# A mixture-of-experts stage: experts two at a time in the two halves of the array's columns, with unsplit fp32 weights

## The chip, the cores and the metric

The kernel runs on one core of a Trainium2 chip. The metric is device time in microseconds (us) of one execution. The kernel before takes 1715.51 us, the median of three runs (1713.52 to 1718.09). One execution was profiled; it took 1711.88 us.

## The reference, cut to what matters

One block of a network over 256 tokens of width 2048, all in float32: an adaptive norm, one projection to three mixers (stick-breaking attention, a state-space layer, a chunked mLSTM), a gated merge, an output projection with a residual, and then the part that the change is about, a hierarchical mixture of experts. A token takes one of 4 groups, and in that group its best 2 of 8 experts:

```python
g_logits = (t @ w_group) + b_group
g_idx = jnp.argmax(g_logits, axis=-1)
e_in_group = jnp.take_along_axis(e_logits, g_idx[:, None, None], axis=1)[:, 0]
top_v, top_i = lax.top_k(e_in_group, TOP_K)
top_w = jax.nn.softmax(top_v, axis=-1) * g_w
...
hid = jax.nn.silu(jnp.einsum('td,edf->tef', t, w1)) * jnp.einsum('td,edf->tef', t, w3)
y = jnp.einsum('tef,efd->td', hid * gates[:, :, None], w2)
...
x = x + gate2 * y          # then a final RMS norm
```

There are 32 experts. Each has w1 and w3 (2048 x 256) and w2 (256 x 2048), 6 MiB in float32, 192 MiB for all of them. The routing depends on the data, so every expert's weights are read.

## The kernel before, in words

Everything up to the output projection (`wo`, which ends at about 1081 us of the profile) is the same in both kernels and is not described here. Weights come from memory in tiles of 1 MiB (128 partitions x 2048 float32), issued on SyncE's queue, and each tile is a buffer of a ring.

**Split products.** A plain float32 product is not used for the large matrices. `split` makes a high part (`hi`, a rounded copy in the type fp32r, made by ScalarE at L134) and a low part (`lo = x - hi`, made by VectorE at L136) of half a tile, 128x1024 at a time. `mm3` (L146 to L148) then issues three fp32r products, high x high, high x low and low x high.

**The experts.** The 256 tokens are put into 128 slots per group: `sel_group` builds a one-hot selection matrix from each token's rank in its group, and `Gather` (rows, scale, turn, finish) picks the tokens by a product with it, scales them, transposes them into 16 chunks of 128 features x 128 slots, modulates and splits them into `XG`. All 8 experts of a group then run over all 128 slots of that group, one expert after the other; a slot whose token did not choose the expert has gate 0. Per expert there are 16 steps (chunks of the 2048 features) of `mm_in`, each with a 128x512 operand that holds w1 and w3 side by side, and 8 steps of `mm_out` (2 chunks of the hidden width x 4 blocks of 512 output columns). One step is one `mm3`, three products. Between the two stand `hidden` (silu, gate, transpose) and `hidden_split`. At the end of a group the result is gated (`gate_rows`, `gate_low`), brought back to the tokens by a product with the transposed selection (`combine_mm`) and added to `x1` (`combine_add`). The gather of the next group and the combine of the last one are spread over the experts of a group in the loop at the end.

**Buffers and order.** `moe_raw` hands out the weight buffers: six in two pools (`st`, which the loads of `wo` use too, and `pd`), and for some of the early tiles the place of other tensors (`Y0`, `Y1`, `H1`). A tile can be loaded again when VectorE has made its last low part. A scheduler orders the instructions of each engine, except in two stretches written out by hand (`manual_schedule`): the router between `wo` and the first expert, and the last expert with the final norm. In the router's stretch the rank of a token in its group needs the group's one-hot `goh` alone; the choice of the two experts is worked out behind it and is needed for the gates alone. If a group has more than 128 tokens, a branch (`overflow`) computes the rest.

Of the kernel before, what the change touches and what calls it, by code (L numbers as in the profile page):

```python
# [18 lines left out]
P = 128  # L19
D = 2048  # L20
# [24 lines left out]
def kernel(ctx: ExitStack, tc: tile.TileContext, A, out, dbg=None):  # L45
# [75 lines left out]
    def split(src, shape, name, part=None, hl=None, buf=None):  # L121

        if part == 1:
            nc.vector.tensor_tensor(out=hl[1], in0=src, in1=hl[0].bitcast(F32), op=ALU.subtract)
            return hl
        hi = buf[0] if buf else ring["pool"].tile([P, 1024], F32R, tag="hi", bufs=ring["bufs"], name=name + "h")
        lo = buf[1] if buf else ring["pool"].tile([P, 1024], F32R, tag="lo", bufs=ring["bufs"], name=name + "l")
# [7 lines left out]
        if part is None:  # L135
            nc.vector.tensor_tensor(out=lv, in0=src, in1=hv.bitcast(F32), op=ALU.subtract)  # L136
# [1080 lines left out]
    slots = {}  # L1217
# [15 lines left out]
    def sel_group(g):  # L1233
        if "sel" not in slots:
            slots["sel"] = pd.tile([P, 2, 4, 128], F32R, tag="wrg", name="sel")
        sel = slots["sel"]
        for tt in range(2):
            V.tensor_scalar(sel[:, tt, g, :], iota, rank[:, tt:tt + 1], oh[:, tt, g:g + 1], op0=ALU.is_equal,
                            op1=ALU.mult)

    def slot_r2(sl, nm):

        pt = psum("ms", f"r2p{nm}")
        for tt in range(2):
            nc.tensor.matmul(pt[:, :1], lhsT=sl[tt].bitcast(F32), rhs=r2[:, tt:tt + 1], start=(tt == 0),
                             stop=(tt == 1))
        r = pd.tile([P, 1], F32, tag="r2s", bufs=2, name=f"r2s{nm}")
        V.tensor_copy(out=r, in_=pt[:, :1])
        return r

    class Gather:


        def __init__(self, sl, nm):
            self.sl, self.nm = sl, nm

        def norms(self):
            if isinstance(self.sl[0], tuple):
                self.sl = [slots["sel"][:, tt, g, :] for tt, g in self.sl]
            self.r = slot_r2(self.sl, self.nm)  # L1260

        def rows(self, j):
            self.pt = psum("ms", f"xg{self.nm}{j}")
            for i in range(2):
                for tt in range(2):
                    nc.tensor.matmul(self.pt, lhsT=self.sl[tt], rhs=xs[i][:, tt, 512 * j:512 * j + 512],
                                     start=(i == 0 and tt == 0), stop=(i == 1 and tt == 1))

        def scale(self, j):
            self.x = pd.tile([P, 512], F32, tag="xgr", bufs=2, name=f"xgr{self.nm}{j}")  # L1270
            nc.scalar.activation(self.x, self.pt, AF.Copy, scale=self.r)

        def turn(self, j):
            self.pT = psum("ms", f"xgT{self.nm}{j}").rearrange("p (k s) -> p k s", k=4)
            for kk in range(4):
                transpose(self.pT[:, kk, :], self.x[:, kk::4], P)

        def modulate(self, j, h):
            for kk in range(4):
                k = 4 * j + kk  # L1280
                if kk % 2 == 0:
                    nc.scalar.activation(h[:, kk, :], self.pT[:, kk, :], AF.Identity, bias=modc[:, 3, k:k + 1],
                                         scale=G2[:, k:k + 1])
                else:
                    V.tensor_scalar(h[:, kk, :], self.pT[:, kk, :], G2[:, k:k + 1], modc[:, 3, k:k + 1],
                                    op0=ALU.mult, op1=ALU.add)

        def finish(self, j, XG):
# [487 lines left out]
```

## Time and profile before

| | us |
|---|---|
| median of 3 runs | 1715.51 |
| the profiled execution | 1711.88 |
| its span, first to last instruction | 1710.1 |
| `wo` ends, router begins | 1080.6 to 1086 |
| first product of an expert | 1097.2 |
| last product of an expert ends | 1692.6 |

Over the whole span PE is busy 94% of the time, VectorE 85%, ScalarE 56%. A matmul's duration in the profile runs from its start to the end of its pipeline, so matmuls overlap, and the distance from one start to the next tells what one costs. The weight loads into the array (PEld) are listed apart.

### The profile page before, as it was taken

What the parts mean: (1) busy time and instruction counts of PE and PEld (TensorE: products, weight loads), DVE (VectorE), ACT (ScalarE), POOL (GpSimd) and SP (SyncE); (2) the same over time, 40 slices, a digit from 0 to 9 for tenths busy, and PEclk for the clock granted to TensorE, in tenths of its full rate; (3) what the DMA queues carried; (4) which work ended last, traced back from release to release, by engine and by line L of the source; (5) the groups of instructions that cost most, each with busy time, mean ns of one, the idle gap of its engine ahead of it and who ended that gap; (6) DMA issues with size and microseconds to landing.
All of it is one profiled execution on the core that took longest, in us unless ns stands there. A gap on an engine that the chain in (4) does not pass through costs nothing. (4 is left out here: it accounts for less than half of the span.)

```text
span 1710.1 us, 26968 instructions
## 1 busy us (share of the span) xinstructions
PE 1613.5 (94%) x10568; PEld 1421.2 (83%) x10568; DVE 1452.8 (85%) x2072; ACT 951.4 (56%) x1133; POOL 38.1 (2%) x59
## 2 busy tenths in 40 slices
PE   1999999999998989989999999899999999999996
PEld 1999998888897988979999988678878877777774
DVE  5889997988799999987788556688898998889897
ACT  4454454755533333424444344577887787777775
POOL 1000010100000000000000100000000000000000
PEclk9999999999999999999999999899999999999998
DMA  9998876677777767777988585598899999899993
GB/s 347 351 358 318 264 210 222 202 247 250 273 278 243 255 237 271 265 244 253 321 314 314 195 316 200 187 361 302 287 361 345 322 338 354 320 327 346 346 350 125
DMA packets 172004, 488.24 MB, mean 286 GB/s; under 512 B 13876, under 2 KB 14048, under 8 KB 162272
## 3 DMA queue, kind: packets, MB, share of 16 engines
q1 hardware_dynamic: 168784, 474.32, 78.3%
q0 software_dynamic: 3088, 12.14, 2.2%
q8 instruction: 84, 1.38, 0.3%
q14 instruction: 48, 0.39, 0.1%
HBM read 479.06 MB, written 6.31 MB: 284 GB/s over the span
## 5 line engine op out<-in xcount | busy, mean ns | idle before, releaser
L136 DVE TENSOR_TENSOR w_1l<-w,w_1h 128x1024 fp32r<-128x1024 f32 x127 | 155.1, 1222 | 20.2 <-ACT w_1h L134 20.0
L136 DVE TENSOR_TENSOR w_0l<-w,w_0h 128x1024 fp32r<-128x1024 f32 x128 | 156.4, 1222 | 17.8 <-ACT w_0h L134 16.4
L321 DVE SCALAR_TENSOR_TENSOR accr<-adar,ccol,accr 128x1024 f32<-128x1024 f32 x120 | 153.5, 1279 | 13.5 <-DMA adar<-in_w_ada_dram 12.4
L134 ACT CAST w_1h<-w 128x1024 fp32r<-128x1024 f32 x128 | 134.5, 1051 | 36.4 <-PE h L148 19.5
L134 ACT CAST w_0h<-w 128x1024 fp32r<-128x1024 f32 x128 | 134.2, 1048 | 24.3 <-PE y L148 14.3
L146 PE MATMUL h<-w_0h,XG 128*128 128x512 f32 x256 | 105.5, 412 | 1.4 <-ACT XG L1292 0.9
L147 PE MATMUL h<-w_0l,XG 128*128 128x512 f32 x256 | 103.0, 402 | 3.7 <-DVE w_0l L136 3.3
L147 PE MATMUL h<-w_1l,XG 128*128 128x512 f32 x256 | 102.4, 400 | 0.2
L148 PE MATMUL h<-w_0h,XG 128*128 128x512 f32 x256 | 101.4, 396 | 0.1
L146 PE MATMUL h<-w_1h,XG 128*128 128x512 f32 x256 | 101.4, 396 | 0.0
L148 PE MATMUL h<-w_1h,XG 128*128 128x512 f32 x256 | 101.1, 395 | 0.0
L136 DVE TENSOR_TENSOR w2s_0l<-w,w2s_0h 128x1024 fp32r<-128x1024 f32 x63 | 77.1, 1224 | 9.0 <-ACT w2s_0h L134 8.6
L136 DVE TENSOR_TENSOR w2s_1l<-w,w2s_1h 128x1024 fp32r<-128x1024 f32 x62 | 75.9, 1224 | 7.9 <-ACT w2s_1h L134 6.2
L301 DVE SCALAR_TENSOR_TENSOR acc<-ada,ccol,acc 128x1024 f32<-128x1024 f32 x60 | 76.9, 1282 | 2.7 <-DMA ada<-in_w_ada_dram 1.4
L134 ACT CAST w2s_1h<-w 128x1024 fp32r<-128x1024 f32 x62 | 65.2, 1052 | 23.7 <-PE y L148 16.6
L134 ACT CAST w2s_0h<-w 128x1024 fp32r<-128x1024 f32 x63 | 66.3, 1052 | 16.0 <-PE h L148 15.6
L147 PEld LDWEIGHTS h<-w_0l,XG 128*128 128x128 f32 x256 | 48.1, 188 | 18.9 <-DVE w_0l L136 9.0
L147 PEld LDWEIGHTS h<-w_1l,XG 128*128 128x128 f32 x256 | 48.1, 188 | 16.5 <-DVE w_1l L136 5.8
L146 PEld LDWEIGHTS h<-w_0h,XG 128*128 128x128 f32 x256 | 48.3, 189 | 12.4 <-ACT XG L1292 1.9
L146 PEld LDWEIGHTS h<-w_1h,XG 128*128 128x128 f32 x256 | 48.1, 188 | 11.5
L148 PEld LDWEIGHTS h<-w_0h,XG 128*128 128x128 f32 x256 | 48.1, 188 | 11.2 <-DVE XG L1293 1.3
L148 PEld LDWEIGHTS h<-w_1h,XG 128*128 128x128 f32 x256 | 48.1, 188 | 10.5
(677 smaller groups left out, 5565.2 us busy)
## 6 DMA issues: line engine op xcount, KB each, us to landing
w<-in_moe_w_dram SPq DMA_DIRECT2D x256, 512.0 KB, 4.9
adar<-in_w_ada_dram SPq DMA_DIRECT2D x64, 1024.0 KB, 5.6
w<-in_moe_w_dram SPq DMA_DIRECT2D x64, 1024.0 KB, 5.6
ada<-in_w_ada_dram SPq DMA_DIRECT2D x64, 512.0 KB, 7.1
g_sb_w<-in_w_in_dram SPq DMA_DIRECT2D x16, 1024.0 KB, 5.6
g_ml_w<-in_w_in_dram SPq DMA_DIRECT2D x16, 1024.0 KB, 5.5
g_s_w<-in_w_in_dram SPq DMA_DIRECT2D x16, 1024.0 KB, 5.5
wo_w<-in_w_out_dram SPq DMA_DIRECT2D x16, 1024.0 KB, 5.1
```

Source lines behind the costliest of these rows:

```text
L134: nc.scalar.copy(out=hv, in_=src)
L136: nc.vector.tensor_tensor(out=lv, in0=src, in1=hv.bitcast(F32), op=ALU.subtract)
L146: nc.tensor.matmul(o, lhsT=lhs[0], rhs=rhs[0], start=start, stop=False, **kw)
L147: nc.tensor.matmul(o, lhsT=lhs[0], rhs=rhs[1], start=False, stop=False, **kw)
L148: nc.tensor.matmul(o, lhsT=lhs[1], rhs=rhs[0], start=False, stop=stop, **kw)
L301: nc.vector.scalar_tensor_tensor(acc, raw[:, :, q], cs, acc, op0=ALU.mult, op1=ALU.add)
L321: nc.vector.scalar_tensor_tensor(acc, raw[:, q], cs, acc, op0=ALU.mult, op1=ALU.add)
```

## The change

It replaces the expert stage from the router on. Experts are paired with experts of the same parity: a set is two neighbouring experts (16 sets), a unit is two sets (8 units), and a slot of a set holds a token that chose either of the set's experts. A unit has 64 slots for its first set and 64 for its second, side by side in the 128 columns of the stationary operand. A `Pair` (16 of them, two per unit) runs one expert of each set at the same time: the first in the array's columns 0 to 63, the second in columns 64 to 127 (`tile_position`), each with its own weights streamed and with plain float32 products on the weights as loaded; nothing of the experts is split any more. There is a step of 16 + 8 per pair, with two products in a step. The overflow branch now begins at 64 tokens in a set and is rewritten. The selection now needs both chosen experts, so their choice moves ahead of the rank in the router's stretch. The ring has 11 weight buffers: three of pool `pd`, three of `st`, three that were the split parts of the projections (`hl`), and two in the place of `H1`. `split` now allocates one tile for both parts. The combine keeps its split products.

```diff
     def split(src, shape, name):
-        hi = buf[0] if buf else ring["pool"].tile([P, 1024], F32R, tag="hi", bufs=ring["bufs"], name=name + "h")
-        lo = buf[1] if buf else ring["pool"].tile([P, 1024], F32R, tag="lo", bufs=ring["bufs"], name=name + "l")
+        hi, lo = (lambda t: (t[:, 0], t[:, 1]))(ring["pool"].tile([P, 2, 1024], F32R, tag="hl", bufs=ring["bufs"],
+                                                                  name=name))
...
+    def sel_unit(u):
+        sel = pd.tile([P, 2, 128], F32R, tag="sel", bufs=2, name=f"sel{u}")
         for tt in range(2):
+            for h in range(2):
+                V.tensor_scalar(sel[:, tt, 64 * h:64 * h + 64], iota[:, 0:64], rank[:, tt, 2 * u + h:2 * u + h + 1],
+                                mem[:, tt, 2 * u + h:2 * u + h + 1].bitcast(F32), op0=ALU.is_equal, op1=ALU.mult)
+        return sel
...
+        def finish(self, j):
+            modulate(self.pT.pop(j), j, self.X[:, 4 * j:4 * j + 4, :])
...
     def moe_raw(name):
+        n = ring_n[0] % 11
+        ring_n[0] += 1
+        if n >= 9:
+            if n == 9:
+                h1[:] = [cp.tile([P, 2, 2048], F32, tag="H1", name=name)]
+            return h1[0][:, n - 9]
+        rp, tag = ((pd, "raw"), (st, "raw"), (ring["pool"], "hl"))[n // 3]
+        return rp.tile([P, 2048], F32, tag=tag, bufs=3, name=name)
...
+        def mm(self, o, lhsT, rhs, start, stop):
+            for h in range(2):
+                sl = slice(64 * h, 64 * h + 64)
+                nc.tensor.matmul(o[sl, :], lhsT=lhsT[:, sl], rhs=rhs(h), start=start, stop=stop,
+                                 tile_position=(0, 64 * h), skip_group_check=True)
+        def mm_in(self, j):
...
+            for kk in range(4):
+                k = 4 * j + kk
+                self.mm(self.ph, self.ga.X[:, k, :], lambda h: self.raw[j][h][:, :, kk, :], k == 0, k == 15)
...
-        gm, ohr = first_max(G, 4, iota4, "g", F32R)
+        gm, oh = first_max(G, 4, iota4, "g")
...
+        v1, oh1 = first_max(eg, 8, iota8, "e1")
...
+        v2, oh2 = first_max(e2, 8, iota8, "e2_")
...
+        V.tensor_reduce(out=m4, in_=both2.rearrange("p t (i q) -> p t i q", q=2), axis=AX.X, op=ALU.max)
+        V.tensor_tensor(out=mem.rearrange("p t (g i) -> p t g i", g=4),
+                        in0=m4[:, :, None, :].to_broadcast([P, 2, 4, 4]),
+                        in1=oh[:, :, :, None].to_broadcast([P, 2, 4, 4]), op=ALU.mult)
         prk = psum("ms", "rank")
+        nc.tensor.matmul(prk[:, 0:16], lhsT=lo_r[:, 0], rhs=mem[:, 0, :], start=True, stop=True)
...
+    for n in range(2 * NU - 1):
+        cur = Pair(n, ga)
...
+        for j in range(4):
+            cur.load_in(j)
+        for f in range(2):
+            cur.load_out(f)
+        cur.mm_in(0)
+        cur.mm_in(1)
+        if gat:
...
+            nxt.rows(2 * el)
+            nxt.scale(2 * el)
+        cur.mm_in(2)
...
+        cur.mm_in(3)
+        cur.hidden()
...
+        for c in range(4):
+            cur.mm_out(0, c, py)
...
+        for c in range(4):
+            cur.mm_out(1, c, py)
```

Of the last pair's w2 the two halves of the output columns come one after the other (`load_out`), as with the last expert before, and its steps, the last combine and the final norm stand in the hand-written stretch at the end.

**Where instructions move.** On PE, before, between the router and the first expert's products (`xg` and `xgT` gather and transpose the tokens; `h` is an expert's hidden product; a number behind `w` names expert, chunk and half):

```order
L1465 MATMUL rank<-goh,lo_r 128x4
...
L262 MATMUL xgT_11258<-cst,xgr_11244 128x128 x3
L146 MATMUL h_11265<-w_0_0_0h,XG_11108 128x512 [waits Activation_49]
L147 MATMUL h_11265<-w_0_0_0l,XG_11108 128x512
L148 MATMUL h_11265<-w_0_0_0h,XG_11108 128x512 [waits DVE_49]
...
L262 MATMUL xgT_11311<-cst,xgr_11289 128x128 [waits DVE_49,Activation_49]
```

On PE now, the same place (`w_0` and `w_2` are the two experts of the first pair, `64x512` is a product in one half of the columns):

```order
L1272 MATMUL xg_10964<-xs_10162,sel_10921 128x512 x2
L1272 MATMUL xg_10964<-xs_10163,sel_10921 128x512 x2
L258 MATMUL xgT_10975<-cst,xgr_10969 128x128 x4
L258 MATMUL xgT_10986<-cst,xgr_10980 128x128 x4
L1293 MATMUL gg_11014<-within,sel_10921 128x8 x2
L258 MATMUL selT_11020<-cst,sel_10921 128x128 x2
L1528 MATMUL cnt<-mem,cst 1x16 x2
L1357 MATMUL h_11063<-w_0_0_11032,XG 64x512
L1357 MATMUL h_11063<-w_2_0_11035,XG 64x512
```

The first expert's products stood between the second and the last chunk of the gather; now all four chunks are turned before the first pair's product. Where three products with full columns stood for one step of one expert, two with half the columns stand for one step of two experts.

On SyncE's queue, before, with what each load waits for (`wo_w` are the projection's tiles; DMAHW is an earlier load's end):

```order
L118 DMA wo_w_11109<-in_w_out_dram 128x4x512 [waits DMAHW4_49,DMAHW1_49,DVE_49]
L1332 DMA w_0_0_11119<-in_moe_w_dram 128x1024 [waits DMAHW5_49,DMAHW2_49,DVE_49]
...
L1332 DMA w_1_0_11447<-in_moe_w_dram 128x1024 [waits DMAHW4_49,DVE_49]
...
L1332 DMA w_2_1_11627<-in_moe_w_dram 128x1024 [waits DMAHW1_49,DVE_49]
...
L1370 DMA w_1_0_11644<-in_moe_w_dram 128x2048 [waits DMAHW3_49,DVE_49,Activation_49]
```

And now, behind the last tile of `wo_w`:

```order
L118 DMA wo_w_10797<-in_w_out_dram 128x4x512 [waits DMAHW7_49,DMAHW2_49,DVE_49]
L1337 DMA w_2_1_11041<-in_moe_w_dram 128x1024 [waits DMAHW0_49,DVE_49]
...
L1337 DMA w_0_3_11050<-in_moe_w_dram 128x1024 [waits PE_49]
...
L1337 DMA w_1_0_11172<-in_moe_w_dram 128x1024 [waits DMAHW1_49,PE_49]
...
L1337 DMA w_3_0_11175<-in_moe_w_dram 128x1024 [waits DMAHW3_49,PE_49]
```

Five tiles stood ahead of this place in the queue before and three now. A load of the steady state waited for VectorE, which reads a tile last; now it waits for PE. The first load that needs a tile back from a pair is that of `w_1_0`, the twelfth tile.

## Rows read from the trace of the kernel before

**Rows 1.** Busy time in stretches of the span. Columns: us of the stretch, then busy time and number of instructions of PE, PEld, DVE, ACT and POOL, the granted share of TensorE's clock, the DMA engines' busy share, GB/s.

```profile
1084.70:1095.00 10.30, 7.33 (x26) 6.16 (x26) 7.15 (x33) 4.75 (x8) 0.00 (x0) 0.50 0.80 295
1110.00:1675.00 565.00, 560.68 (x2455) 445.76 (x2456) 506.66 (x524) 436.30 (x508) 0.23 (x1) 1.00 0.92 335
...
1250.00:1300.00 50.00, 49.96 (x220) 39.77 (x219) 47.50 (x49) 40.42 (x47) 0.00 (x0) 1.00 0.99 366
0.00:100.00 100.00, 63.03 (x463) 58.36 (x464) 70.67 (x73) 48.92 (x62) 5.91 (x14) 1.00 0.98 349
```

**Rows 2.** Waits of SyncE's queue in the expert stage (1110 to 1680): who waited for whom, us in total, times, longest.

```profile
SPq L1332 <- DVE w_1l L136: 198.5, 83, 8.9
SPq L1370 <- DVE w2s_1l L136: 114.3, 45, 3.7
```

**Rows 3.** The page's DMA issues of the experts' weights: line, count, KB each, median us from issue to landing.

```profile
w<-in_moe_w_dram SPq DMA_DIRECT2D x256, 512.0 KB, 4.9
...
w<-in_moe_w_dram SPq DMA_DIRECT2D x64, 1024.0 KB, 5.6
```

**Rows 4.** PE's instructions in order of time, in the expert stage: start us, duration us, engine, line, operation. Eight products of an expert, fp32r, 512 columns streamed.

```profile
1396.06 0.40 PE L147 MATMUL y<-w2s_0l,hh 128*128 128x512 f32 x1
...
1397.69 0.40 PE L148 MATMUL y<-w2s_1h,hh 128*128 128x512 f32 x1
```

**Rows 5.** The same view at 397 us, plain fp32 products on the full array. One product makes two records, merged here (x2).

```profile
397.54 0.60 PE L867 MATMUL rest<-sbs,cst 128*128 128x256 f32 x2
397.97 0.38 PE L868 MATMUL rest<-sbs,cst 128*128 128x128 f32 x2
398.19 0.39 PE L869 MATMUL rest<-sbs,cst 128*128 128x128 f32 x2
```

**Rows 6.** The same view at 759 us, plain fp32 products in four groups of 32 columns (128*32): x8 is four products with two records each, one product per column group.

```profile
758.79 0.39 PE L670 MATMUL yc<-u_sb,KB 128*128 128x128 f32 x2
759.10 0.43 PE L675 MATMUL yc<-bu,C 128*32 128x128 f32 x8
759.34 0.40 PE L679 MATMUL yc<-bu,C 128*32 128x127 f32 x8
759.56 0.40 PE L675 MATMUL yc<-bu,C 128*32 128x128 f32 x8
759.78 0.40 PE L679 MATMUL yc<-bu,C 128*32 128x127 f32 x8
760.11 0.38 PE L146 MATMUL g_ml_b<-hT,g_ml_w_1h 128*128 128x256 f32 x1
```

**Rows 7.** Loads of the stationary operand, by source line: count, duration ns min/median/max, first and last start, form (partitions*columns).

```profile
L274 PEld LDWEIGHTS adar<-accr,cst x128: 106/120/130, 371.0 to 939.8; 128*32 128x32 f32 x128
...
L146 PEld LDWEIGHTS h<-w_0h,XG x256: 186/188/202, 1097.2 to 1679.3; 128*128 128x128 f32 x128
```

**Rows 8.** All engines in order of time, from the end of `wo` to the first expert (in brackets: idle time before it and what ended it).

```profile
1080.60 0.39 PE L148 MATMUL wo_b<-wo_w_1h,mh 128*128 128x512 f32 x1
...
1086.33 0.16 DVE L1224 TENSOR_REDUCE gmx<-lg 128x2 f32<-128x8 f32 x1
1086.52 0.17 DVE L1227 TENSOR_TENSOR goh<-lg,gmx 128x8 fp32r<-128x8 f32 x1
...
1087.12 0.17 DVE L1230 TENSOR_TENSOR goh<-goh,gmn 128x8 fp32r<-128x8 f32 x1
...
1087.43 0.34 PE L1465 MATMUL rank<-goh,lo_r 128*128 128x4 f32 x1 [2.03 <-DVE goh L1230]
...
1088.75 0.60 DVE L1238 TENSOR_SCALAR sel<-cst,rank_t,goh 128x128 fp32r<-128x128 f32 x2
...
1090.02 3.76 PE L1266 MATMUL xg<-xs,sel 128*128 128x512 f32 x8
...
1092.16 0.69 ACT L1271 ACTIVATE xgr<-xg,r2s 128x512 f32<-128x512 f32 x1 [4.38 <-PE xg L1266]
...
1094.67 0.46 ACT L1282 ACTIVATE hg<-xgT,modc,G 128x128 f32<-128x128 f32 x1
1095.16 0.41 DVE L1285 TENSOR_SCALAR hg<-xgT,G,modc 128x128 f32<-128x128 f32 x1 [2.17 <-ACT hg L1282]
...
1096.12 0.40 DVE L1285 TENSOR_SCALAR hg<-xgT,G,modc 128x128 f32<-128x128 f32 x1
...
1097.22 0.50 PE L146 MATMUL h<-w_0h,XG 128*128 128x512 f32 x1 [0.94 <-ACT XG L1292]
```

**Rows 9.** The same view at the end of the span.

```profile
1674.77 0.53 POOL L1701 DMA_DIRECT2D fg<-in_final_g_dram  x1 [592.20 <-DVE w2s_1l L136]
...
1681.83 0.38 ACT L1353 ACTIVATE s<-h 128x256 f32<-128x256 f32 x1 [0.80 <-PE h L148]
...
1683.40 0.37 ACT L1363 CAST hh<-hT 128x256 fp32r<-128x256 f32 x1 [0.25 <-PE hT L262]
...
1692.23 0.40 PE L148 MATMUL y<-w2s_3h,hh 128*128 128x512 f32 x1
...
1700.70 5.39 DVE L1746 SCALAR_TENSOR_TENSOR x<-x,r,fg 128x512 f32<-128x512 f32 x8 [0.91 <-DVEq L1571]
1701.48 4.97 SPq L1748 DMA_DIRECT2D out_dram<-x  x8
```

More of the change, by code (lines that the diff above doesn't have):

```diff
@@ L1275, in turn @@
+            x = self.x.pop(j)
             for kk in range(4):
[L1276 to L1286, printed above, removed]
@@ new lines, in back @@
+        def back(self):
+            pt = psum("ms", f"selT{self.u}")
+            for tt in range(2):
+                transpose(pt[:, 128 * tt:128 * tt + 128], self.sel[:, tt].bitcast(F32), P)
+            self.selT = pd.tile([P, T], F32R, tag="selT", bufs=2, name=f"selTs{self.u}")
+            nc.scalar.copy(out=self.selT, in_=pt[:, :T])
+    ring_n = [0]
+    h1 = []
+    def moe_raw(name):
+        n = ring_n[0] % 11
[6 more added lines that the diff above has]
+        return rp.tile([P, 2048], F32, tag=tag, bufs=3, name=name)
@@ new lines @@
+    done = nxt = None
+    for n in range(2 * NU - 1):
+        cur = Pair(n, ga)
+        u, el = cur.u, cur.el
+        gat = u + 1 < NU
+        for j in range(4):
+            cur.load_in(j)
+        for f in range(2):
+            cur.load_out(f)
+        cur.mm_in(0)
+        cur.mm_in(1)
+        if gat:
+            if el == 0:
+                nxt = Gather(u + 1)
+                nxt.norms()
+                nxt.gates()
+            nxt.rows(2 * el)
+            nxt.scale(2 * el)
+        cur.mm_in(2)
+        if gat:
+            nxt.rows(2 * el + 1)
+            nxt.scale(2 * el + 1)
+        cur.mm_in(3)
+        cur.hidden()
+        if done is not None:
+            combine_add(2 * el, combine_mm(done[0], done[1][el][:, 0], u - 1, 2 * el))
+        elif gat:
+            nxt.turn(2 * el)
+        cur.hidden_turn()
+        if done is not None and gat:
+            nxt.turn(2 * el)
+        if gat:
+            nxt.finish(2 * el)
+        if el == 0:
+            py = [psum("mm", f"y{u}_{c}") for c in range(4)]
+        for c in range(4):
+            cur.mm_out(0, c, py)
+        if gat:
+            nxt.turn(2 * el + 1)
+            nxt.finish(2 * el + 1)
+        if done is not None:
+            combine_add(2 * el + 1, combine_mm(done[0], done[1][el][:, 1], u - 1, 2 * el + 1))
+        for c in range(4):
+            cur.mm_out(1, c, py)
+        if el == 1:
+            yp = row_pairs(u)
+            for c in range(4):
+                gate_low(yp[c // 2][:, c % 2], gate_rows(py[c], yp[c // 2][:, c % 2], u, c))
+            done = ga.selT, yp
+            ga = nxt
+            ga.back()
@@ L1700 @@
+    cur = Pair(2 * NU - 1, ga)
+    for j in range(4):
+        cur.load_in(j)
+    for f in range(2):
+        cur.load_out(f)
     fg = pd.tile([P, D], F32, tag="raw", bufs=3, name="fg")
```

517 lines of the change are left out of this document (189 added, 328 removed).

## Prediction

> **What bounds the kernel now.** I read the windows by stage first, then the waits of the load queue, then PE's timeline, because the question is whether the expert stage ends by products or by loads. In the 565 us of that stage PE is busy 560.7, the DMA engines have a share of 0.92 and move 335 GB/s [rows 1]. Busy PE is not PE at its peak, so I take the distance of starts: 1396.06 to 1397.69 over seven products is 0.233 us each [rows 4]. An expert has 24 steps of three products, 32 experts 2304; times 0.233 is 537 us of the 595 from the first product at 1097.2 [rows 8] to the end of the last at 1692.6 [rows 9]. Gather, transposes and combine fill most of the rest. PE is the bound.
>
> The loads are close behind. All experts are 192 tiles of 1.0486 MB, 201.3 MB, in the issues of [rows 3]. The load queue waits for VectorE's low parts, 198.5 us and 114.3 us [rows 2]: the loads run at the pace at which tiles come free, not at their own. Left alone they go faster: 366 GB/s at share 0.99 in 1250 to 1300, and 349 at 0.98 in the first 100 us [rows 1].
>
> **The change part by part.** *The step.* Three fp32r products per expert and step go, 1.40 us for two experts. One plain fp32 product per expert comes. Its price is in [rows 5]: 256 streamed columns take 397.54 to 397.97, 0.43 us for two records; 128 take 0.22. So 512 columns cost 0.86 us. Whether the two halves overlap is the heart of the case. In [rows 6] four products of 128 columns, each in its own quarter of the array's columns, start every 0.22 us (759.34, 759.56, 759.78), the time that one such product takes alone. Four ran in the time of one, so I take two in the time of one: 0.86 us per step of two experts.
>
> *PE per pair.* 24 steps by 0.86 are 20.6 us. Eight gather products and eight of the combine at 0.233 are 3.7. Eight gather transposes and two of the hidden product come to 1.7 (an estimate: 0.11 a record from [rows 5], with the pipeline's start). Norms, gates and the transposed selection are 0.8, estimated. Changing between full and half columns costs about 0.1: 758.79 to 759.10 is 0.31 for one product that takes 0.22, and 759.78 to 760.11 is 0.33 for a wave that takes 0.22 [rows 6]. A pair has five such blocks, so ten changes, 1.0 us. From the start of the silu to the end of the copy of the transposed product there are 1.9 us [rows 9], of which the combine's products cover half. Sum 28.8 us.
>
> *Loads per pair.* Twelve tiles are 12.58 MB. Between 335 and 366 GB/s they take 37.6 to 34.4 us. I take 360, near the faster row, since its packets are these weights' own and the first 100 us carry another matrix: 35.0 us. This exceeds 28.8, so the bound passes from PE to the loads, with 6 us to spare per pair, and the removed splits (1.05 us on ScalarE and 1.22 on VectorE per half tile) are worth nothing beyond the earlier release of tiles. PE releases two tiles at the end of each four steps, 3.4 us after they can start; eleven buffers hold 32 us of loads, so the queue is not starved by it.
>
> The Trainium skill, "DMA: Bandwidth & Descriptors", section Specifications, puts the memory limit of one core at about 358 GB/s. The 366 GB/s over 50 us in [rows 1] lie above it. By the page the stage would end 3 us later than by my 360.
>
> *The start.* The loads are full speed only once tiles come back. Eleven tiles can be loaded before a pair has computed; the last five of them wait for the projection's last product at 1080.6 [rows 8], and at 2.9 us each they are in at about 1096. Then the queue waits for the twelfth. The router grows: the choice of the two experts, its sum and its maximum, 16 small VectorE instructions in a row, come ahead of the rank, at the 0.2 us spacing of 1086.33, 1086.52 and 1087.12 (two intervals there) [rows 8], 3.2 us. A unit's selection is four instructions of 64 columns for two of 128 (0.6 us together), between 0 and 0.6 more; I take 0.5. The gather thus begins at 1090.0 + 3.7 = 1093.7. Before, the first expert's product came 7.2 us after the gather's first (1090.02 to 1097.22), behind two turned chunks; now it stands behind four. A chunk is finished by alternating ScalarE and VectorE, 1094.67 to 1096.52, 1.85 us; with the scaling 2.0 per chunk, and 4.0 for two. First pair product at 1104.9; its first four steps end at 1108.3, and the first two tiles are free. Of this neither end is certain: 1104 if the chunks overlap better, 1112 if the clock, 0.50 of full from 1084.7 to 1095.0 [rows 1], stays there through these steps.
>
> *The stream.* 181 tiles are left, 189.8 MB. At 360 GB/s 527.2 us; at 366, 349 and 335 it is 518.6, 543.8 and 566.6. Add 2 us for the restart (4.9 us from issue to landing under load [rows 3] less the transfer's own share) and 2 us for the final norm's 1 MB, which joins at the end as before [rows 9]. Loads end at 1108.3 + 2 + 527.2 + 2 = 1639.5.
>
> *The tail.* With the last tile in, two blocks of output columns are left, 3.4 us, and one combine between them, 0.9. From the end of the last product to the end of the span is 1710.1 - 1692.6 = 17.5 us [rows 9]; this part keeps its instructions. For a lowered clock in a thinly used stretch I add 1.0. The span ends at 1662.3. The profiled execution is 1.8 us longer than its span, so 1664.1, and lies 3.6 below the median of the runs: 1667.7, said as 1668.
>
> **The rivals.** *The halves do not overlap.* Two products in a step then take 1.72 us, a pair 28.8 + 20.6 = 49.4, the stage 1104.9 + 16 x 49.4 = 1895, with the tail 1913, and 1919 as a median. That is slower by 12%. The kernel would be slower from the point where a step costs over 1.18 us (stage end 1692.6 less 1104.9, over 16, less 8.2 us of other work, over 24). For it: only groups of 32 columns with 128 streamed are seen here, never 64 with 512. Against it: three of three spacings in [rows 6]. 6%.
>
> *Loads of the stationary operand are not hidden.* Each step needs two of them in a row per half. A load of 32 columns takes 0.12 us and one of 128 takes 0.188 [rows 7]; 64 lie between. At 0.188 a pair gains 24 x 2 x 0.188 = 9.0 us, 37.8 in all, and the stage would last 605 us from 1104.9: about 1733 as a median. At 0.12 it is 34.6, just under the loads, and the forecast stands. Against it: in [rows 6] waves of products with fresh stationary operands follow at 0.22, with no room for a load between. 5%. The Trainium skill, "TensorE: Matmul & The Clock Gate", Part 3, says that such a load overlaps with running products only where the row groups differ; here both halves use the same rows, so by that rule this rival is the result, and [rows 6] speak against the rule.
>
> *Loads stay at their present pace or under it.* At 330 GB/s the stream takes 575 us and the median is 1716, no change; at 335 it is 1707. For it: 335 is what the stage shows now, and tiles of a pair are freed two at a time. Against it: the reason for that pace is named in [rows 2] and goes. No change 5%; what lies between 335 and 360 belongs to the forecast.
>
> *PE falls to half its clock through the stage*, since it idles in every pair. Then 24 steps take 41 us and PE is the bound at some 53 us per pair. But a PE that is the bound is busy all the time, and in the stretches where it was that the clock was 1.00 [rows 1], so this undoes itself. 3%, slower.
>
> *The branch for over 64 tokens runs.* It would read all weights twice more. The reference's router on its inputs puts 18 to 37 tokens into a set, so it does not; under 1%.
>
> **How the numbers follow.** The forecast, a load-bound stage, has 81%, with its own range of 1650 to 1707 (first tiles free at 1104 and 366 GB/s; 335 GB/s). With the rivals that end beyond it the 80% range is 1645 to 1708. What a measurement of this kernel can tell from no change is about 0.3%, 5 us. Faster by more than that: 81% and the milder half of the hidden-load rival and of the slow-load rival, 85%. Within: 5%. Slower: 10%, from the first, the second and the clock rival.
>
> **What would show it.** Right: two starts of 64-column products within some ns of each other or one record apart, a step of 0.86 us in the timeline; DMA share 0.97 or more from 1110 to 1640; PE waiting for DMA in every pair; the load queue waiting for PE. The gap in the loads before the first pair ends at about 1108, and the last weight lands at about 1640. Wrong: PE busy without idle time and the DMA share under 0.95 (a step over 1.1 us, or loads into the array in the way), or a load stream with gaps that begin after 1110.

## The result, and the profile after

The changed kernel takes 1613.97 us, the median of four runs (1612.8 to 1614.76), against 1715.78 us for the kernel before (four runs, 1713.52 to 1718.09). The ratio is 0.9406, with a 95% interval of 0.939 to 0.9422. It is faster, as forecast, but by 102 us instead of 48: the time lies 54 us under the forecast and 31 us under the lower end of its range. The profiled execution took 1612.8 us, with a span of 1611.0.

The windows of the kernel after (stretch, its length, then the busy time and instructions of PE, PEld, VectorE, ScalarE and GpSimd, the granted clock, the DMA share and GB/s) answer to [rows 1]:

```profile
1095.00:1100.00 5.00, 5.00 (x16) 4.02 (x16) 0.83 (x4) 1.61 (x3) 0.00 (x0) 0.50 0.07 28
...
1110.00:1580.00 470.00, 454.61 (x1918) 180.86 (x1914) 106.03 (x222) 75.64 (x150) 0.00 (x0) 1.00 1.01 404
1200.00:1500.00 300.00, 288.32 (x1211) 116.09 (x1208) 73.14 (x155) 50.39 (x101) 0.00 (x0) 1.00 1.01 404
...
1578.00:1580.00 2.00, 2.00 (x12) 0.48 (x8) 0.00 (x0) 0.00 (x0) 0.00 (x0) 1.00 0.72 289
1580.00:1581.00 1.00, 1.00 (x6) 0.67 (x4) 0.07 (x1) 0.39 (x1) 0.19 (x1) 1.00 0.12 49
```

VectorE falls from 506.66 us of the stage to 106.03, ScalarE from 436.30 to 75.64. The loads move 404 GB/s at share 1.01, where [rows 1] show 335 at 0.92, and the last weight is in at about 1580. Around 1100 the queue idles with all eleven tiles in. PE still looks busy, 454.61 us of 470.

The waits of the load queue (engine and line, what it waited for: us in all, times, longest) answer to [rows 2], and the issues (count, size, median us to landing) to [rows 3]:

```profile
SPq L1337 <- DMA w<-in_moe_w_dram: 85.2, 92, 2.1
SPq L1337 <- PE h L1357: 83.6, 46, 4.7
SPq L1351 <- PE h L1357: 71.3, 14, 8.3
SPq L1351 <- PE y L1357: 46.5, 22, 4.0
SPq L1351 <- DMA w<-in_moe_w_dram: 20.6, 24, 1.1
SPq L1337 <- PE y L1357: 17.4, 11, 4.1
```

```profile
w<-in_moe_w_dram SPq DMA_DIRECT2D x256, 512.0 KB, 9.6
...
w<-in_moe_w_dram SPq DMA_DIRECT2D x64, 1024.0 KB, 10.5
```

Nothing waits for VectorE's low parts any more. Two thirds of what the queue waits for is products that free a tile, the rest its own earlier loads. A load of 512 KB lands 9.6 us after its issue instead of 4.9, so several are under way at once. In the waits of PE from 1110 to 1580, the only large one is for the gated hidden product `s`, which PE transposes; no load stands among them:

```profile
PE hT L258 <- DVE s L1370: 14.0, 15, 1.0
PE xg L1272 <- DVE r2s L1266: 1.4, 5, 0.3
```

The beginning of the stage, from the timeline (start, us, engine, line, operation), answers to [rows 8], its end to [rows 9]:

```profile
1095.12 3.76 PE L1272 MATMUL xg<-xs,sel 128*128 128x512 f32 x8
...
1105.68 6.73 PE L1357 MATMUL h<-w,XG 128*64 128x512 f32 x30
...
1109.36 0.33 SPq L1351 DMA_DIRECT2D w<-in_moe_w_dram  x1
...
1583.62 5.37 PE L1357 MATMUL y<-w,hh 128*64 128x512 f32 x24 [0.52 <-ACT hh L1379]
1588.92 1.19 PE L1406 MATMUL sc<-yp,selTs 128*128 128x512 f32 x4
1590.05 1.94 PE L1357 MATMUL y<-w,hh 128*64 128x512 f32 x8
```

Beside the forecast's own numbers:

| | forecast | measured |
|---|---|---|
| gather begins | 1093.7 | 1095.1 |
| first product of a pair | 1104.9 | 1105.7 |
| two tiles free, the queue resumes | 1108.3 | 1109.4 |
| last weight in (without the norm's 1 MB) | 1637.5 | about 1580 |
| end of the span | 1662.3 | 1611.0 |

The start is 1.1 us late, the stream of 181 tiles takes 470.6 us instead of 529.2, and from the last weight to the end there are 31.0 us instead of 24.8: 1.1 - 58.6 + 6.2 = -51.3. The stream is the term that failed.

### The profile page after: what moved, and what is told of

It is laid out like the page before. It is cut to its first block, busy times and chain, and to the rows that moved or that the text cites. A ratio compares the mean times of both kernels' runs of the same rounds, so it can differ in the third digit from the quotient of the medians.

```text
span 1611.0 us, 24587 instructions
## 1 busy us (share of the span) xinstructions
PE 1496.7 (93%) x10000; PEld 1143.2 (71%) x10000; DVE 1034.7 (64%) x1759; ACT 574.2 (36%) x756; POOL 38.2 (2%) x59
## 5 line engine op out<-in xcount | busy, mean ns | idle before, releaser
L1357 PE MATMUL h<-w,XG 128*64 128x512 f32 x1024 | 243.6, 596 | 0.0
L1357 PEld LDWEIGHTS h<-w,XG 128*64 128x64 f32 x1024 | 75.1, 137 | 138.1 <-issue 136.5
L1357 PE MATMUL y<-w,hh 128*64 128x512 f32 x512 | 150.4, 598 | 0.5 <-ACT hh L1379 0.5
L1415 DVE TENSOR_TENSOR x<-x,sc 128x512 f32<-128x512 f32 x64 | 43.0, 683 | 108.9 <-PE sc L1406 108.9
L1357 PEld LDWEIGHTS y<-w,hh 128*64 128x64 f32 x512 | 49.0, 136 | 81.5 <-issue 77.3
L144 PE MATMUL g_sb_b<-hT,g_sb_w 128*128 128x256 f32 x256 | 73.1, 286 | 3.1 <-DVE g_sb_w L132 3.1
L144 PE MATMUL g_ml_b<-hT,g_ml_w 128*128 128x256 f32 x256 | 73.0, 285 | 2.0 <-DVE g_ml_w L132 2.0
L142 PE MATMUL g_ml_b<-hT,g_ml_w 128*128 128x256 f32 x256 | 73.2, 286 | 0.0
L142 PE MATMUL g_sb_b<-hT,g_sb_w 128*128 128x256 f32 x256 | 72.7, 284 | 0.0
L143 PE MATMUL g_ml_b<-hT,g_ml_w 128*128 128x256 f32 x256 | 72.6, 284 | 0.0
L143 PE MATMUL g_sb_b<-hT,g_sb_w 128*128 128x256 f32 x256 | 72.4, 283 | 0.0
L142 PE MATMUL g_s_b<-hT,g_s_w 128*128 128x256 f32 x256 | 71.9, 281 | 0.0
L143 PE MATMUL g_s_b<-hT,g_s_w 128*128 128x256 f32 x256 | 71.7, 280 | 0.0
L144 PE MATMUL g_s_b<-hT,g_s_w 128*128 128x256 f32 x256 | 71.5, 279 | 0.1
L132 DVE TENSOR_TENSOR wo_w<-wo_w,wo_w 128x1024 fp32r<-128x1024 f32 x32 | 39.0, 1223 | 31.8 <-ACT wo_w L131 31.5
L131 ACT CAST wo_w<-wo_w 128x1024 fp32r<-128x1024 f32 x32 | 33.7, 1053 | 59.1 <-PE wo_b L144 43.7
```

Source lines behind the costliest of these rows:

```text
L131: nc.scalar.copy(out=hv, in_=src)
L142: nc.tensor.matmul(o, lhsT=lhs[0], rhs=rhs[0], start=start, stop=False, **kw)
L143: nc.tensor.matmul(o, lhsT=lhs[0], rhs=rhs[1], start=False, stop=False, **kw)
L144: nc.tensor.matmul(o, lhsT=lhs[1], rhs=rhs[0], start=False, stop=stop, **kw)
L1357: nc.tensor.matmul(o[sl, :], lhsT=lhsT[:, sl], rhs=rhs(h), start=start, stop=stop, tile_position=(0, 64 * h), skip_group_check=True)
L1415: V.tensor_tensor(out=x1[:, tt, sl], in0=x1[:, tt, sl], in1=pts[tt], op=ALU.add)
```

## The experiments

Two questions stand behind that term. Why were the loads of the kernel before slower, at 335 GB/s and at 366 in its fullest stretch? And what sets the pace of 404 now: the loads, or PE? All times below are medians. Each group of runs was timed beside the kernel before on one chip (1714 to 1717 us), and not all groups on the same one, so a difference of 2 or 3 us between groups tells nothing.

### Extra work on VectorE and ScalarE, a ring of 6, and two prices

The first theory (A) is that the splits' traffic slowed the loads; the second (B) that too few loads were queued. For A, work like the splits', on constant data:

```diff
+    def extra(k):
+        for i in range(2 * k):
+            V.tensor_tensor(out=dv, in0=gb2[:, 0:512], in1=gb2[:, 512:1024], op=ALU.subtract)
+            nc.scalar.copy(out=da, in_=gb2[:, 0:512])
```

> The changed kernel with 28 subtractions on VectorE and 28 rounding copies on ScalarE (128x512 each, on constant data, into scratch tiles that nothing reads) added per pair, so that both engines are about as busy as with the splits of the kernel before (some 85% and 74%); the loads, products and the ring of 11 are untouched. Theory A (traffic of VectorE and ScalarE in SBUF slowed the loads of the kernel before): the loads of the stage fall from 404 GB/s to about 366 to 375, the last weight lands 35 to 47 us later, and the time is 1650 to 1660. Theory B (too few loads were queued, so the start of each was not hidden): the rate stays at 400 or more and the time at 1612 to 1625.

It took 1706.2 us, which neither theory had. Its windows say why:

```profile
1140.00:1200.00 60.00, 56.95 (x243) 22.84 (x242) 54.05 (x92) 55.42 (x98) 0.00 (x0) 0.92 0.96 385
1200.00:1500.00 300.00, 234.54 (x903) 91.67 (x903) 260.38 (x420) 211.89 (x368) 0.00 (x0) 0.84 0.78 304
```

From 1140 to 1200 VectorE and ScalarE are busy 90 and 92% and the loads move 385 GB/s at share 0.96, 401 per unit of share, where the changed kernel has 414 at 1.02 in the same stretch (406 per unit): work of the two engines as such does not slow the loads, and A is out in this form. VectorE reading the loaded tiles themselves was not tried alone. The time went elsewhere, first of all into PE's longest wait:

```profile
PE hT L258 <- DVE s L1370: 71.2, 16, 9.9
```

The extra work stood ahead of the gating of the hidden product, for which PE waited 71.2 us in all (14.0 in the changed kernel). It also stood ahead of the router: PE waited 20.2 us for `mem` (5.8), and the first pair began at 1120.7 instead of 1105.7. With these pauses its granted clock, a mean of the levels 1.2 and 2.4 GHz, fell to 0.84. How the 92 us divide between waits and clock is not shown: the profiled execution took 1717.7 us at a mean clock of 0.912, the other eight of this kernel 1703.7 to 1708.0 at 0.956 to 0.958.

For B, six of the eleven buffers:

```diff
-        n = ring_n[0] % 11
+        n = ring_n[0] % 6
...
-        rp, tag = ((pd, "raw"), (st, "raw"), (ring["pool"], "hl"))[n // 3]
+        rp, tag = ((pd, "raw"), (st, "raw"))[n // 3]
```

> The changed kernel with a ring of 6 weight buffers in place of 11. Five tiles fewer are in before the first pair, some 13 us under either theory. Theory A: when the DMA engines are busy they still move 400 GB/s or more (GB/s divided by share), and what is lost is idle time, share under 0.95. Theory B: GB/s divided by share falls to 365 to 385 as in the kernel before, because the packets at the start of a load take longer; the landing time falls from 9.6 us for 512 KB to about 5; the time is 1650 to 1680.

1630.2 us, with 395 GB/s at share 0.99 from 1200 to 1500 and landings of 8.1 us. So the number of buffers alone was not it either: of the 16 us some 13, by an estimate, are the five tiles that are not in before the first pair, at 2.6 us each (1 MiB at 404 GB/s).

Then two prices. Both products of a step over all columns:

```diff
-                nc.tensor.matmul(o[sl, :], lhsT=lhsT[:, sl], rhs=rhs(h), start=start, stop=stop,
-                                 tile_position=(0, 64 * h), skip_group_check=True)
+                nc.tensor.matmul(o, lhsT=lhsT, rhs=rhs(h), start=start and h == 0, stop=stop and h == 1)
```

> The changed kernel with each of the two products of a step over all 128 columns of the array (both experts of a pair then run over all 128 slots and are summed, so the expert part of the output is changed), the same number of products, loads and buffers. It prices the overlap of the two halves. If halves run side by side, as the forecast took it: a step goes from 0.86 to 1.72 us, a pair from about 30 to 49.4 us, the median is 1900 to 1925. If the halves did not run side by side, or something else sets the pace, the time stays within 5% of 1614. The rate of the loads falls to about 255 GB/s with the queue waiting for products.

1874.3 us: the halves do run side by side, and that is worth 260 us. From the first pair product at 1105.6 to the last weight load of `y` at 1852.5 (its groups: `1105.6 to 1834.3`, `1137.9 to 1852.5`) a pair takes 46.7 us on average. And half the loads:

```diff
-            for e in self.es:
+            for e in self.es[:1]:
...
-                self.mm(self.ph, self.ga.X[:, k, :], lambda h: self.raw[j][h][:, :, kk, :], k == 0, k == 15)
+                self.mm(self.ph, self.ga.X[:, k, :], lambda h: self.raw[j][0][:, :, kk, :], k == 0, k == 15)
```

> The changed kernel with one weight tile for both halves (the second expert of each pair uses the weights of the first, so the expert part of the output is changed): half the loads, the same products. It shows what PE needs by itself. By the forecast's 28.8 us per pair the last product ends at 1105 + 461 = 1566 and the median is about 1588. If PE is as much the bound as the loads now, 29.5 us or more per pair and 1600 to 1614. If PE needs clearly less than 28.8 per pair, under 1580.

1560.6 us, the third case: PE alone needs less than was forecast. Its timeline in a pair:

```profile
1312.46 0.44 PE L258 MATMUL hT<-cst,s 128*128 128x128 f32 x2
...
1313.36 3.65 PE L1357 MATMUL y<-w,hh 128*64 128x512 f32 x16
...
1318.55 3.65 PE L1357 MATMUL y<-w,hh 128*64 128x512 f32 x16
...
1340.91 0.44 PE L258 MATMUL hT<-cst,s 128*128 128x128 f32 x2
...
1367.95 0.44 PE L258 MATMUL hT<-cst,s 128*128 128x128 f32 x2
```

Two pairs lie between 1312.46 and 1367.95: PE needs 27.7 us for one. The 24 steps are 20.6 of that, at 0.86 us each. Averaged over all pairs as above, half the loads take (1538.5 - 1104.0) / 16 = 27.2 us (groups `1104.0 to 1526.7`, `1123.3 to 1538.5`); the price with full columns, 46.7 - 27.2 = 19.5 more, is about the 24 steps once again.

### What slows a load: one start on an empty queue

Neither A nor B in its first form held, so B was sharpened: a load that finds the queue empty pays for its start, and the share counts that as busy. A ring of about four, a ring of two:

```diff
-        n = ring_n[0] % 11
+        n = ring_n[0] % 4
...
+        return (pd, st)[n - 2].tile([P, 2048], F32, tag="raw", bufs=3, name=name)
```

> The changed kernel with a ring that lets about four tiles be loading or waiting at a time (two in the place of H1, one of pool pd, one of st, in turn), no extra work on VectorE or ScalarE. The ring of 6 kept 395 GB/s at share 1.00, so buffers alone did not slow the loads, and the extra work kept 308 GB/s at share 0.79 (390 per unit of share); but half the loads gave 228 at 0.63 (362) and full columns 267 at 0.70 (381), with landings of 4.3 and 5.1 us. Theory B in its sharper form (a load that finds the queue empty pays its start, and the share counts that as busy): with four tiles the queue often runs dry, 512 KB land in 4 to 5.5 us, GB/s divided by share is 360 to 385, and the time is 1660 to 1710, some 18 us of it from seven tiles fewer before the first pair. Rival (the queue does not matter): GB/s divided by share stays at 395 or more and what is lost shows as share under 0.9 with the landing time unchanged.

> The changed kernel with a ring of 2 tiles, so never more than one step's two tiles are loading, and the queue runs empty for each. Theory B: 512 KB land in 4.5 us or less and GB/s divided by share is 355 to 372, as in the kernel before and with half loads, though VectorE and ScalarE have little to do. Rival (the number of queued loads does not matter to the packets): GB/s divided by share stays at 390 or more. Each step is then a load of two tiles (5.1 us and some 2 us of latency) followed by 3.4 us of products, about 10.5 us, 96 times: a median of 2080 to 2200 under either.

The first took 1720.7 us (324 GB/s at 0.83, landing in 6.8: the queue was not as short as meant), the second 2348.0 (168 at 0.44, landing in 4.9). Per unit of share that is 390 and 382: between theory and rival both times. But with one number per kernel a pattern shows. One more run tests it: the kernel with full columns, its steps turned so that one tile comes free at a time.

```diff
-            for kk in range(4):
-                k = 4 * j + kk
-                self.mm(self.ph, self.ga.X[:, k, :], lambda h: self.raw[j][h][:, :, kk, :], k == 0, k == 15)
+            for h in range(2):
+                for kk in range(4):
+                    k = 4 * j + kk
+                    self.mm(self.ph, self.ga.X[:, k, :], lambda h: self.raw[j][h][:, :, kk, :], k == 0, k == 15, h)
```

> The kernel with full columns again (products over all 128 columns, PE the bound, the expert part of the output changed in the same way), with the order of the products turned so that one tile's four steps run before the other's, and a tile is released every 3.4 us instead of two every 6.9. Theory B with a price per start: where the queue runs empty each start costs the 16 engines about 0.3 us that the share counts as busy, whatever follows it; one start per tile in the kernel before gave 364 GB/s per unit of share and with half loads 362, one per two tiles 381 (full columns) and 382 (ring of 2), none 400 to 410. So here 358 to 370 at a rate of 262 to 270 GB/s, and 512 KB land in 3.5 to 4.6 us instead of 5.1. Rival (it is not the starts): 378 to 385 as with full columns. The time is that of full columns under either, 1865 to 1885.

1875.1 us, with 268 GB/s at 0.74. Its windows, and those of the kernel with full columns as it was:

```profile
1200.00:1500.00 300.00, 299.61 (x811) 146.01 (x810) 46.44 (x102) 32.69 (x64) 0.00 (x0) 1.00 0.74 268
```

```profile
1200.00:1500.00 300.00, 299.59 (x810) 145.72 (x809) 46.72 (x102) 33.10 (x64) 0.00 (x0) 1.00 0.70 267
```

The same bytes at the same pace, and a higher share. The kernel before and half loads, the other two with one start per tile, have in the same stretch:

```profile
1200.00:1500.00 300.00, 298.04 (x1312) 237.56 (x1311) 271.00 (x287) 234.57 (x279) 0.00 (x0) 1.00 0.92 333
```

```profile
1200.00:1500.00 300.00, 300.00 (x1378) 118.10 (x1376) 84.31 (x178) 59.05 (x116) 0.00 (x0) 1.00 0.63 228
```

The kernels side by side, from 1200 to 1500 (landing of 512 KB: median of the whole run):

| kernel | GB/s, share | GB/s per unit of share | landing, us |
|---|---|---|---|
| before | 333, 0.92 | 362 | 4.9 |
| half loads | 228, 0.63 | 362 | 4.3 |
| full columns, one tile at a time | 268, 0.74 | 362 | 4.3 |
| full columns, two tiles at a time | 267, 0.70 | 381 | 5.1 |
| ring of 2 | 168, 0.44 | 382 | 4.9 |
| ring of about 4 | 324, 0.83 | 390 | 6.8 |
| extra work | 304, 0.78 | 390 | 7.6 |
| kernel before with one product (below) | 390, 0.99 | 394 | 7.5 |
| ring of 6 | 395, 0.99 | 399 | 8.1 |
| after | 404, 1.01 | 400 | 9.6 |
| paired order (below) | 413, 1.02 | 405 | 10.2 |

One tile at 362 counts 2.90 us and at 405 2.59; two tiles at 381 count 5.50, at 405 5.18. Either way a start costs about 0.3 us of counted time. The run with one tile at a time is the test of it, since it changes only how tiles come free; that the kernel before and half loads, with and without splits, agree at one start per tile speaks for it too. What happens inside a start no run here shows.

Last, the kernel before itself, with its ring and ScalarE's high parts, but one product instead of three and no low parts on VectorE (rounded weights):

```diff
-                mm3(self.ph, (self.XG[0][:, k, :], self.XG[1][:, k, :]),
+                mm1(self.ph, (self.XG[0][:, k, :], self.XG[1][:, k, :]),
```

> The kernel before with only the first of the three products of each expert step, high by high, and without VectorE's low parts of the weights (the expert part of the output is rounded, so it is less exact): ring, loads, ScalarE's high parts, gather and combine as before. PE's work in the stage falls to about a third and the loads become the bound. Theory B (the loads of before were slow per unit of share because products set the pace, a full ring let one tile go at a time, and each load began on an almost empty queue): with the same ring, now mostly empty, the queue is deep, 512 KB land in 7 us or more, the stage runs at 390 to 410 GB/s at share 0.97 or more, and the median is 1600 to 1640. Rival (something in the kernel before itself holds its loads to 366 GB/s: ScalarE's work on the tiles, the pools of the ring): share 0.97 or more at 350 to 372 GB/s, and a median of 1650 to 1680.

1618.9 us, as B expected, with these windows and landings of 7.5 us:

```profile
1120.00:1560.00 440.00, 323.97 (x920) 174.46 (x920) 73.94 (x146) 386.00 (x478) 0.00 (x0) 0.79 1.00 398
```

398 GB/s with the buffers of the kernel before, and ScalarE busy 88% with the loaded tiles. So neither 335 nor 366 was what the loads can do. The run takes away VectorE's low parts together with the products; that the products set the pace of 335 is read from [rows 1] (PE busy 560.68 of 565 us, VectorE 506.66) and not separated by a run. The 366 at share 0.99, 370 per unit of share, fits a queue that restarts at almost every tile.

### The start and the tail

Three edits of the start: two more first tiles in the places `Y0` and `Y1`; the first pair's first eight steps between the gather's last chunks; both.

```diff
+        if n in (11, 12):
+            return pd.tile([P, 2048], F32, tag=f"Y{n - 11}", name=name)
```

```diff
         ga.finish(1)
+        first.mm_in(0)
         ga.turn(2)
         ga.scale(3)
         ga.finish(2)
+        first.mm_in(1)
         ga.turn(3)
```

> The changed kernel with the two places Y0 and Y1, which are not needed until the second pair ends, as tiles 12 and 13 of the first loads. If the stage is bound by the loads from its start to its end, two tiles of 2.56 us move into the 13 us in which the queue idles, and the time falls by 5 us to about 1609. If products are the bound, or the tail takes it back: no change, 1612 to 1615.

> The changed kernel with the first pair's first two groups of four steps put between the gather's last chunks (behind the finish of chunk 1 and of chunk 2) instead of behind all four. The first product moves from 1105.7 to about 1101, the queue resumes at about 1105 instead of 1109.8. Load-bound stage: 4 to 5 us less, about 1609.5. If products are the bound: also about 4 less, since they start earlier; if the products in the way hold up the gather: no change or up to 3 us more.

> The changed kernel with both of the former edits. Load-bound stage with its idle stretch cut from both sides: the two gains add, 9 to 10 us less, about 1604. If only the start of the products matters, as with the early pair alone, about 1609.5.

They took 1611.7, 1611.4 and 1608.8 us. The first two overlap the runs of the changed kernel (up to 1614.6 and 1613.6 against 1612.8 and more), so no gain is shown for either edit alone; both together gain some 4 to 5 us, half of what was expected. The profiled executions say the same once the time ahead of the stage is taken off, which differs by some us from one execution to the next: the last product of `wo` starts at 1082.3 in the changed kernel and at 1080.6, 1079.6 and 1080.6 in these, and from there to the end of the span it is 528.8 us against 527.9, 529.2 and 525.0. With the early pair alone the loads run at 354 GB/s and share 0.94 from 1110 to 1140, where the changed kernel has 393 at 1.00: they begin earlier, and then wait for tiles. On the last of the three the tail, with the combines of the last pair moved forward:

```diff
-            if j >= 2:
-                c = j
+            if j < 2:
+                c = j + 2
```

> The changed kernel with 13 first tiles and the early first pair as before, and the two combines that the last pair does behind its third and fourth group of steps done behind its first and second, where PE waits for loads anyway. In the run before, silu and gate of the last pair came 1.5 us late because VectorE was adding that combine. If the stage is load-bound to its end: 1.5 to 2.5 us less than 1608.8, so 1606 to 1607.5. If the tail is bound by the last tile of w2: no change, 1608 to 1609.5.

1608.9 us, no change. Its timeline shows PE without a pause, not a wait for loads: the work only changed places.

```profile
1564.24 1.21 PE L1409 MATMUL sc<-yp,selTs 128*128 128x512 f32 x4
1565.38 3.65 PE L1360 MATMUL h<-w,XG 128*64 128x512 f32 x16
1568.97 1.20 PE L1409 MATMUL sc<-yp,selTs 128*128 128x512 f32 x4
1570.10 7.09 PE L1360 MATMUL h<-w,XG 128*64 128x512 f32 x32
```

### The order of PE's products

So PE was looked at again. In the changed kernel two pairs take 1368.71 - 1305.53 = 63.2 us, 31.6 each, 3.9 more than with half the loads:

```profile
1305.53 0.44 PE L258 MATMUL hT<-cst,s 128*128 128x128 f32 x2 [1.03 <-DVE s L1370]
...
1306.43 4.56 PE L1357 MATMUL y<-w,hh 128*64 128x512 f32 x16
1310.92 0.75 PE L258 MATMUL xgT<-cst,xgr 128*128 128x128 f32 x4
...
1312.52 4.13 PE L1357 MATMUL y<-w,hh 128*64 128x512 f32 x13
...
1317.87 2.08 PE L1272 MATMUL xg<-xs,sel 128*128 128x512 f32 x8
```

```profile
1368.71 0.44 PE L258 MATMUL hT<-cst,s 128*128 128x128 f32 x2 [1.03 <-DVE s L1370]
```

Four steps of `y` take 4.49 us (1306.43 to 1310.92) and, with half a step of `h` among them, 5.35 (1312.52 to 1317.87), against 3.59 with half the loads (1313.36 to 1316.95, and 1318.55 to the next at 1322.14). The queue of PE tells why. The scheduler put the products of one expert's w2 tile ahead of the other's (`w2_9`, then `w2_11`):

```
L1357 MATMUL y2_0_11749<-w2_9_1_11813,hh5_11878 64x512
L1357 MATMUL y2_1_11750<-w2_9_1_11813,hh5_11878 64x512
L1357 MATMUL y2_2_11751<-w2_9_1_11813,hh5_11878 64x512
L1357 MATMUL y2_3_11752<-w2_9_1_11813,hh5_11878 64x512
L1357 MATMUL y2_0_11749<-w2_11_1_11815,hh5_11878 64x512
L1357 MATMUL y2_1_11750<-w2_11_1_11815,hh5_11878 64x512
```

Four products in a row use one half of the array, and the other half gets its first one only behind them. The transposes of the hidden product also lost the combine that covered their wait with half the loads, and now wait 1.03 us. The test keeps the program's own order on PE, which restores both at once, with the new kernel and with the edited start:

```diff
+    with tc.manual_schedule(engines={ENG.PE}):
         for n in range(2 * NU - 1):
             cur = Pair(n, ga)
```

> The changed kernel with PE's instructions of the expert loop kept in the order of the program (the two experts' products side by side) instead of the scheduler's. If that order was the bound: a pair needs 27.7 us of PE as with half the loads, the loads become the bound at about 410 GB/s, 30.7 us a pair instead of 31.6, PE waits for loads, and with the products closer behind the last load the tail shortens too: 10 to 18 us less than 1614, so 1596 to 1604. If the loads were the bound already: 1611 to 1616 and the same rate.

> The kernel with 13 first tiles and the early first pair (1608.8), with PE's order kept in the loop as well. If the order was the bound, the edits of the start now count in full as well, 9 to 10 us on top of the gain of the order: 1587 to 1595. If the loads were the bound: 1606 to 1610.

The first took 1601.0 us (ratio 0.9344 to the kernel before, 0.9327 to 0.9361), 13 less than the changed kernel, in the range of the theory. Some 10 of them are the order's: the ratios differ by 10.6 us, and from the last product of `wo` to the end of the span the profiled executions take 518.6 and 528.8. Its windows, and its waits on PE and on the queue:

```profile
1200.00:1500.00 300.00, 288.52 (x1260) 120.15 (x1256) 75.52 (x161) 52.97 (x104) 0.00 (x0) 1.00 1.02 413
```

```profile
PE h L1357 <- DMA w<-in_moe_w_dram: 18.6, 15, 1.5
```

```profile
SPq L1337 <- DMA w<-in_moe_w_dram: 262.9, 218, 3.4
...
SPq L1337 <- PE h L1357: 13.6, 10, 3.8
```

PE waits for loads now, the queue waits for its own loads instead of for products, and 413 GB/s at share 1.02 is the loads' own pace here. The second took 1597.3 us (0.932, 0.9303 to 0.9336), the fastest kernel here, but 3.7 us better than the first instead of 9 to 10. Two windows of its profiled execution (1600.2 us, where the other three took 1596.3 to 1598.1) point at where the rest stayed:

```profile
1110.00:1140.00 30.00, 28.95 (x144) 11.74 (x140) 4.83 (x18) 6.43 (x12) 0.00 (x0) 1.00 0.95 366
...
1570.00:1575.00 5.00, 5.00 (x20) 1.56 (x18) 1.07 (x2) 1.38 (x3) 0.00 (x0) 0.74 0.09 33
```

Loads that begin earlier run at 366 GB/s until 1140 (403 in the first kernel), as in the run with the early pair alone, and PE's clock fell to 0.74 in the tail (1.00 in the first). This is read from the rows of one execution; no run separates it.

## Why the prediction was right and wrong

**The step of two experts: right.** 0.86 us was forecast for 24 steps; four steps take 3.59 us with the change of columns, where the two experts stand side by side in the queue, and full columns cost 19.5 us a pair more. The rival of halves that don't overlap is out.

**Loads of the stationary operand: right, they are hidden.** One of 64 columns takes 0.137 us (the groups `128*64 128x64`), and a pair with half the loads 27.7 us in all, 20.6 of them steps, with no room for 96 loads (13.2 us, or 6.6 when those of the two halves run at the same time). In the changed kernel they do, two in 0.14 us, while the products of `y` run from 1583.62 on:

```profile
1584.10 0.14 PEld L1357 LDWEIGHTS y<-w,hh 128*64 128x64 f32 x2 [0.29 <-issue]
```

The Trainium skill, "TensorE: Matmul & The Clock Gate", Part 3, has such loads overlap only where the row groups differ; here both halves use the same rows, and the trace disagrees.

**PE per pair: the sum was near, the order was overlooked.** 28.8 us was forecast and 27.7 is what the program's order needs (half loads). In the changed kernel it is 31.6, because in up to 8 of the 24 steps the two experts' products don't stand side by side, and because the transposes wait 1.03 us. A count of steps doesn't see that; the order of the queue decides it.

**The stream: the step that failed.** It is "Between 335 and 366 GB/s they take 37.6 to 34.4 us. I take 360, near the faster row", and with it "Left alone they go faster: 366 GB/s". A pair's 12.58 MB take 30.5 us at the 413 GB/s of the paired order, not 35.0, and the last weight came 58 us early. The rows were read as a limit because their share was 0.99. By the price found above, that share counts a start on an empty queue as busy, one per tile, while the products let the loads go one at a time. The lower bound of 335 was a pace set by the products, and the upper one of 366 was no upper bound. A rate above it belonged in the range: the 4.9 us to landing in [rows 3], against 9.6 in the kernel after, say that little was under way. The Trainium skill, "Perfetto Trace Analysis", section Roofline, says that one core alone can pass its share of 358 GB/s and puts a practical ceiling at about 120% of it; the prediction weighed the 358 alone. The 413 GB/s here are 115%, and the trace agrees.

**"The bound passes from PE to the loads": not quite.** At 31.6 us a pair, against 30.5 for the loads, PE remained the bound by about a microsecond; the sign "PE waiting for DMA in every pair" is missing in the changed kernel and there with the paired order. With the right numbers for both, 27.7 and 30.5, the forecast's own picture would have been that kernel, at 1601.

**Start: right within 1.4 us. Tail: 6.2 us short.** The forecast had PE wait for the last tile with two blocks of columns left. PE was behind: when the last weight was in, at 1580, it had just ended the steps of `h`, and all four blocks of `y` were to come, 12 us to the last product at 1592.0 instead of 4.3. Another 1.5 us were lost behind the last product; the 2 us for the norm's 1 MB and the 1.0 for the clock were not used.

The side and the chance (0.85 for faster) were right, the range too narrow below: it was closed at 366 GB/s. One sum is off without changing that: a first tile free at 1104 and 366 GB/s give 1667.7 - 4.3 - 8.6 = 1655, where the forecast's own range begins at 1650.

## What to carry to other kernels

A DMA rate measured while products set the pace is not the rate of the loads, even at a share of 0.99. Look at the landing time and at what the queue waits for: if it waits for products and lands quickly, its rate is theirs, and its share holds the restarts.

Where two operations must meet to overlap, as two halves of the array, read the order of the queue that issues them. Here the scheduler undid part of a pairing that the program had written, and keeping the written order brought 10 us or more in 1614.

## What was not expected of the hardware

- One core loaded 413 GB/s for 300 us (1200 to 1500 with the paired order), at share 1.02.
- A load issued to an empty queue costs about 0.3 us that the share shows as busy (362, 381 and 405 GB/s per unit of share with one start per tile, one per two tiles, and hardly any).
- VectorE and ScalarE at 90 and 92% for 60 us, on constant data, did not slow the loads: 401 GB/s per unit of share, 406 without.
- With waits of up to 9.9 us on PE, one in a pair, its mean granted clock was 0.84 over 300 us of the profiled execution (0.912 over its whole span; 0.956 to 0.958 in the other eight); the kernel before with a third of the products, whose PE is busy 74% of the time, had 0.79, while its loads held 398 GB/s.
